# Queries and keys written twice before their transposes, and a shorter inverse root, in a hybrid decoder step

## The chip, the cores and the metric

The kernel runs on one core of a Trainium2 chip. The metric is the device time of one execution in microseconds. Times inside a profile count from the start of its span. The engines are called TensorE (PE in the rows; PEld is its weight load), VectorE (DVE), ScalarE (ACT), GpSimd (POOL) and SP, which issues most of the transfers.

## What is computed

One layer for 1,024 prompt tokens and 8 x 4 sample tokens of width 1,024. A root-mean-square norm feeds one input projection to queries, keys, values, a gate and the inputs of a state-space branch; the two branches' outputs go through one output projection and are added to the input. The change lies in the attention branch: four heads, each with two softmax maps of 64 columns, whose queries and keys are normed each for itself:

```python
q = _rmsnorm(q.reshape(b, L, N_HEADS, 2, QK_DIM), q_g)
k = _rmsnorm(k.reshape(b, L, N_HEADS, 2, QK_DIM), k_g)
s = jnp.einsum('bqhcd,bkhcd->bhcqk', q, k) * (QK_DIM ** -0.5)
...
w = p[:, :, 0] - lam * p[:, :, 1]
```

The normed keys are also an output of the layer.

## The kernel before, in words

Matrix products are made with operands split into a high and a low part: a 32-bit number is written to a narrower format (fp32r) by ScalarE and the remainder by VectorE, and high x high, high x low and low x high are summed by TensorE in PSUM.

The program has three stages. The first (`first_phase`) norms the tokens and runs the state-space branch; `stats` (L288) there makes the inverse root of each token's mean square. The second goes through the four heads. The third is the output projection (`out_proj`), whose first row blocks are mixed with the last head's attention.

In the second stage `project` runs, for each head, over four steps of 256 tokens (j = 0 to 3). Each step makes 48 matmuls of 128x512 into two PSUM tiles `acc` (three exist): columns 0 to 255 are the queries and keys of the head's two maps, then values and gate. `norm_qk` (L832) takes both tiles: sums of squares on ScalarE, the inverse root `rsqrt` (L155) on VectorE, and the multiply from PSUM into the tile `qn` (L848). Some time later `keep_qkv` (L899), here called a keep, turns `qn` by transposes on TensorE (L907) into a PSUM tile `tr`, of which two exist, and writes the step's tile `pt`: for each map the scaled query's high part and low part, each on partitions 0 to 63 and again on 64 to 127, and the keys with their high part on one half of the partitions and their low part on the other (L916 to L921). So one matmul of contraction 128 gives high x high + high x low. The plain keys `kf` go out by a transfer (L922).

The attention of the same and the previous head is interleaved with this by hand: `mix` draws from generators by rates and delays given in microseconds of an estimate, and a scheduler then orders each engine's queue by its own estimate of durations. `scores` multiplies `pt` tiles into the PSUM tiles `sc` (two), adds the bias and takes the minimum on VectorE (L1030), the exponential on ScalarE (L1035), and joins the two maps (L1040). `values` transposes the joined weights (L1055, tile `tr`), copies them out (L1058) and multiplies by the values (tile `pv`). `attn_norm` norms the result with another `rsqrt` (L1084 writes `o`), `attn_out` transposes it (L1091, tile `tr`). `sample_attend` does the eight sample groups with paged keys and values. Weights of the next head are split meanwhile, the low parts in turn on VectorE and GpSimd (L183). Each engine takes its queue in order.

The functions that the diff touches, and what calls them:

Of the kernel before, what the change touches and what calls it, by code (L numbers as in the profile page):

```python
# [9 lines left out]
F32 = mybir.dt.float32  # L10
F32R = mybir.dt.float32r
I32 = mybir.dt.int32
AF = mybir.ActivationFunctionType
OP = mybir.AluOpType
# [10 lines left out]
QD = 64  # L25
# [4 lines left out]
BIG = 1e30  # L30
NBUCK = 32
# [95 lines left out]
class Kernel:  # L127
# [27 lines left out]
    def rsqrt(self, out, x, tmp):  # L155
        v = self.nc.vector
        v.tensor_scalar(tmp.bitcast(I32), x.bitcast(I32), 1, None, op0=OP.logical_shift_right)
        v.tensor_scalar(out.bitcast(I32), tmp.bitcast(I32), -1, 0x5F3759DF, op0=OP.mult, op1=OP.add)
        for _ in range(3):
            v.scalar_tensor_tensor(tmp, out, -0.5, out, op0=OP.mult, op1=OP.mult)  # L160
            v.tensor_tensor(tmp, tmp, x, op=OP.mult)
            v.scalar_tensor_tensor(out, tmp, 1.5, out, op0=OP.add, op1=OP.mult)
# [669 lines left out]
    def norm_qk(self, accs, n, ve):  # L832
# [4 lines left out]
        qn = self.att.tile([128, 2, 256], F32, name="qn", tag="qn", bufs=2)  # L837
# [9 lines left out]
        for i, a in enumerate(accs):  # L847
            v.tensor_tensor(qn[0:n, i].rearrange("p (c d) -> p c d", d=QD), a[0:n, 0:256].rearrange("p (c d) -> p c d", d=QD),  # L848
                            r[0:n, 4 * i:4 * i + 4][:, :, None].to_broadcast([n, 4, QD]), op=OP.mult)
        return qn  # L850

    def project(self, w):
# [3 lines left out]
        for h in range(NH):  # L856
            st = {"ga": {}, "PT": {}, "V": {}, "kept": {}, "out": set()}
            self.heads.append(st)
            for j in range(4):
# [25 lines left out]
                qn = self.norm_qk(accs, 128, [self.xe[:, 2 * j + i:2 * j + i + 1] for i in range(2)])  # L885
# [13 lines left out]
    def keep_qkv(self, h, j, qn, vo, st):  # L899
        nc = self.nc  # L900
        v, g = nc.vector, nc.gpsimd
        pt = st["PT"][j] = self.pt("pt")
        nc.sync.dma_start(self.O["v_p"][256 * j:256 * j + 256, 128 * h:128 * h + 128].rearrange("(i p) c -> p i c", i=2), vo)
        qk = self.tr()
        for x in range(2):
            for i in range(2):
                nc.tensor.transpose(qk[:, 256 * x + 128 * i:256 * x + 128 * i + 128], qn[:, i, 128 * x:128 * x + 128], self.idn)  # L907
        q, k = qk[:, 0:256], qk[:, 256:512]
        kf = self.att.tile([128, 256], F32, name="kf", tag="kf", bufs=1)
        half = [slice(64 * c, 64 * c + 64) for c in range(2)]  # L910
        with self.tc.high_priority(HP2):

            for c, ps in enumerate(half):
                hi, lo, kk = (pt[:, 512 * z + 256 * c:512 * z + 256 * c + 256] for z in range(3))
                ot = half[1 - c]
                nc.scalar.activation(hi[ps], q[ps], AF.Copy, scale=self.gains[ps, 0:1])  # L916
                v.tensor_copy(hi[ot], hi[ps].bitcast(F32))  # L917
                v.scalar_tensor_tensor(lo[ps], q[ps], self.gains[ps, 0:1], hi[ps].bitcast(F32), op0=OP.mult, op1=OP.subtract)  # L918
                v.tensor_copy(lo[ot], lo[ps].bitcast(F32))
                nc.scalar.activation(kk[half[0]], k[ps], AF.Copy, scale=self.pkc("k_g")[ps])  # L920
                v.scalar_tensor_tensor(kk[half[1]], k[ps], self.pkc("k_g")[ps], kk[half[0]].bitcast(F32), op0=OP.mult, op1=OP.subtract)  # L921
            nc.scalar.activation(kf, k, AF.Copy, scale=self.pkc("k_g"))  # L922
        nc.sync.dma_start(self.O["kT"][h, :, 256 * j:256 * j + 256], kf)
        st["kept"][j] = self.clock
# [424 lines left out]
def _build(arrays):  # L1349
    import concourse.bacc as bacc  # L1350

    nc = bacc.Bacc("TRN2", target_bir_lowering=False, num_devices=1)
# [29 lines left out]
```

## Time and profile before

| what | value |
|---|---|
| median of three runs | 678.12 us (677.19 to 678.22) |
| profiled execution | 676.66 us |
| its span | 674.9 us |
| mean granted clock of TensorE | 0.944 of full speed |
| busy, TensorE, VectorE, ScalarE, GpSimd | 595.2, 489.1, 313.7, 160.2 us |

Busy time is the union of the times that an engine's instructions were shown as running, over the whole span. A matmul's shown time overlaps that of the next one, so the rate of a row of matmuls is read from starts, or from the chain of waits, and not from their mean duration. The chain of waits is followed back from the last instruction; each piece is either work or the wait that ended last. The span is 1.76 us shorter than the profiled execution's time, and that execution 1.46 us shorter than the median.

### The profile page before, as it was taken

How to read it: one execution, taken by the hardware profiler on the slowest of the kernel's cores; microseconds unless marked ns; L12 is line 12 of the kernel's file. 1: busy time of each engine (PE TensorE's matmuls, PEld its weight loads, DVE VectorE, ACT ScalarE, POOL GpSimd, SP SyncE). 2: the span in 40 equal slices, each digit the busy share in tenths (PEclk: the TensorE clock that was granted, in tenths of full speed). 3: DMA queues.
4: the chain of work that ended last, by engine and by line, in shares of the span. 5: the costliest groups of instructions: out<-in, count | busy, mean ns of one | idle time of the engine just before them, and what ended most of it. 6: DMA issues, size and time to landing. Idle time of an engine off the chain costs nothing.

```text
span 674.9 us, 11323 instructions
## 1 busy us (share of the span) xinstructions
PE 595.2 (88%) x3490; PEld 493.2 (73%) x3490; DVE 489.1 (72%) x1639; ACT 313.7 (46%) x984; POOL 160.2 (24%) x165
## 2 busy tenths in 40 slices
PE   5927679568698999989999899998999989999997
PEld 4926579568687887768877688776887757887775
DVE  5978998899775337899668996689966899922111
ACT  6952332121363336676456764567645677411000
POOL 0681679777524400030000300003000020001000
PEclk9967779797978999999999999999999998999999
DMA  9754408352256450243002530024300166333221
GB/s 305 264 157 130 103 21 219 99 158 67 87 189 171 156 169 17 62 142 110 24 25 62 146 105 25 26 61 146 105 17 31 55 188 214 110 120 124 83 82 51
DMA packets 85738, 74.64 MB, mean 111 GB/s; under 512 B 8685, under 2 KB 74766, under 8 KB 85678
## 3 DMA queue, kind: packets, MB, share of 16 engines
q1 hardware_dynamic: 83374, 69.51, 34.0%
q10 hardware_dynamic: 2304, 4.41, 1.8%
q8 instruction: 28, 0.46, 0.3%
q14 instruction: 32, 0.26, 0.1%
HBM read 53.85 MB, written 20.04 MB: 109 GB/s over the span
## 4 chain that ended last, share of the span: by engine, by line
PE 44%; DVE 30%; ACT 7%; DMA 7%; POOL 6%; issue 5%; SPq 1%; POOLq 0%; DVEq 0%; ACTq 0%
PE acc L135 30%; PE sc L135 5%; PE pv L135 4%; DVE s L1030 3%; DMA xtok<-in_x 2%; DVE ws L183 2%; PE tr L1055 2%; DVE pt L918 2%; DMA gz<-gsd 1%; DVE pt L921 1%; PE tr L135 1%; POOL gz L477 1%; DVE E_im L511 1%; DVE et L507 1%; DVE pt L917 1%
## 5 line engine op out<-in xcount | busy, mean ns | idle before, releaser
L135 PE MATMUL acc<-ws,xt 128*128 128x512 f32 x768 | 204.5, 403 | 0.2 <-DVE gz L501 0.2
L135 PEld LDWEIGHTS acc<-ws,xt 128*128 128x128 f32 x768 | 137.1, 189 | 25.7 <-issue 1.2
L183 POOL TENSOR_TENSOR ws<-wraw,ws 128x512 fp32r<-128x512 f32 x30 | 46.8, 1563 | 369.4 <-ACT ws L180 289.0
L135 PE MATMUL acc<-xt,ws 128*128 128x352 f32 x576 | 99.3, 332 | 8.0 <-ACT ws L180 8.0
L135 PEld LDWEIGHTS acc<-xt,ws 128*128 128x128 f32 x576 | 95.3, 194 | 10.8 <-ACT ws L180 8.4
L135 PE MATMUL acc<-ws,o 128*128 128x512 f32 x336 | 84.5, 400 | 2.9 <-ACT ws L180 0.9
L135 PEld LDWEIGHTS acc<-ws,o 128*128 128x128 f32 x336 | 63.2, 192 | 17.4 <-ACT ws L180 1.3
L1035 ACT ACTIVATE s<-s,mn 128x128 f32<-128x128 f32 (+7 forms) x64 | 49.6, 778 | 28.7 <-DVE mn L1030 18.8
L135 PE MATMUL sc<-pt 128*128 128x256 f32 (+1 forms) x320 | 58.0, 296 | 5.0 <-DVE mn L1030 2.6
L135 PEld LDWEIGHTS sc<-pt 128*128 128x128 f32 x320 | 46.0, 189 | 21.7 <-DVE mn L1030 5.3
L180 ACT ACTIVATE ws<-wraw 128x512 fp32r<-128x512 f32 x68 | 41.8, 627 | 34.5 <-PE acc L135 22.5
L1264 DVE TENSOR_TENSOR xres<-acc,xres 128x512 f32<-128x512 f32 x16 | 11.0, 690 | 51.8 <-PE acc L135 51.8
L135 PE MATMUL pv<-vo,wt 128*128 128x128 f32 x288 | 42.0, 284 | 0.0
L135 PEld LDWEIGHTS pv<-vo,wt 128*128 128x128 f32 x288 | 37.9, 196 | 4.0 <-ACT wt L1058 1.9
L183 DVE TENSOR_TENSOR ws<-wraw,ws 128x512 fp32r<-128x512 f32 x38 | 31.7, 837 | 6.2 <-ACT ws L180 6.1
L405 ACT ACTIVATE acc<-gs 128x352 f32<-128x352 f32 x12 | 5.6, 468 | 61.3 <-DVE gs L404 61.3
L135 PE MATMUL acc<-z,ws 128*128 128x352 f32 x144 | 25.9, 340 | 4.4 <-DVE gs L406 2.7
L135 PEld LDWEIGHTS acc<-z,ws 128*128 128x128 f32 x144 | 24.7, 199 | 5.6 <-DVE gs L406 2.9
L1055 PE MATMUL tr<-cn,s 128*128 128x128 f32 x144 | 26.9, 279 | 1.3 <-ACT kf L922 1.3
L840 ACT ACTIVATE qn<-acc 128x64 f32<-128x64 f32 x128 | 26.8, 225 | 0.0
L1030 DVE CUSTOM_DVE_ANT_0 s<-sc,cb 128x512 f32<-128x512 f32 (+3 forms) x48 | 26.3, 549 | 0.5
L1040 DVE SCALAR_TENSOR_TENSOR s<-s,ls 128x128 f32<-128x128 f32 (+7 forms) x32 | 26.0, 813 | 0.3
(281 smaller groups left out, 1084.1 us busy)
## 6 DMA issues: line engine op xcount, KB each, us to landing
wraw<-in_w_in SPq DMA_DIRECT2D x44, 256.0 KB, 3.2
xT<-in_xT SPq DMA_DIRECT2D x12, 352.0 KB, 7.3
xtok<-in_x SPq DMA_DIRECT2D x8, 512.0 KB, 5.3
cached<-in_cache_k SPq DMA_DIRECT2D x64, 64.0 KB, 1.9
cached<-in_cache_v SPq DMA_DIRECT2D x64, 64.0 KB, 1.9
wraw<-in_w_out SPq DMA_DIRECT2D x16, 256.0 KB, 2.9
xres<-in_x SPq DMA_DIRECT2D x16, 256.0 KB, 3.0
out_y<-xres SPq DMA_DIRECT2D x16, 256.0 KB, 2.0
```

The source lines that it names most:

```text
L135: self.nc.tensor.matmul(out, lhsT, rhs, start=start, stop=stop)
L180: nc.scalar.activation(hi, raw, AF.Copy)
L183: (nc.vector if self.turn else nc.gpsimd).tensor_tensor(lo, raw, hi.bitcast(F32), op=OP.subtract)
L477: nc.gpsimd.tensor_tensor(gz, gz, z, op=OP.mult)
L507: eng.tensor_tensor(t1, a_im, b_im, op=OP.mult)
L840: nc.scalar.activation(qn[0:n, i, 64 * c:64 * c + 64], a[0:n, 64 * c:64 * c + 64], AF.Square, accum_out=ss[0:n, 4 * i + c:4 * i + c + 1])
L918: v.scalar_tensor_tensor(lo[ps], q[ps], self.gains[ps, 0:1], hi[ps].bitcast(F32), op0=OP.mult, op1=OP.subtract)
L1030: v.tensor_tensor_reduce(out=s[:, k0 + a0:k0 + a1], in0=q[:, a0:a1], in1=bias, op0=OP.add, op1=OP.min, scale=1.0, scalar=last, accum_out=m)
L1035: nc.scalar.activation(s[:, 0:L], s[:, 0:L], AF.Exp, bias=last, scale=-1.0, accum_out=ls[:, 2 * i + c:2 * i + c + 1])
L1040: v.scalar_tensor_tensor(wv, st[1][:, 0:L], cf, wv, op0=OP.mult, op1=OP.add)
L1055: nc.tensor.transpose(q[:, 128 * b:128 * b + 128], wv[:, 128 * (b0 + b):128 * (b0 + b) + 128], self.idn)
L1264: v.tensor_tensor(x, a, x, op=OP.add)
```

## The change

`norm_qk` gets a factor `times`. For the prompt it is 2: `qn` has 512 columns per token block in place of 256, each 64-column map standing there twice in a row. A keep makes eight transposes into two PSUM tiles, one for the queries and one for the keys, so that each map stands on both halves of the partitions as it leaves TensorE. The high and low parts of the queries are then written by one instruction each over 128 partitions and 512 columns, the keys by one instruction of that size and one of 64 x 512, and `kf` by two of 64 x 256; the copies from one half of the partitions to the other (L917, L919) are gone. The sample group keeps `times=1`.

`rsqrt` goes from eleven vector instructions to eight: the integer start value in one instruction in place of two, then one Newton step with changed constants and one step of higher order in place of three Newton steps. It is called for the tokens, the queries and keys, the attention's output and the sample groups.

The scratch for dynamic DMAs is set to 2,048 bytes.

```diff
     def rsqrt(self, out, x, tmp):
         v = self.nc.vector
-        v.tensor_scalar(tmp.bitcast(I32), x.bitcast(I32), 1, None, op0=OP.logical_shift_right)
-        v.tensor_scalar(out.bitcast(I32), tmp.bitcast(I32), -1, 0x5F3759DF, op0=OP.mult, op1=OP.add)
-        for _ in range(3):
-            v.scalar_tensor_tensor(tmp, out, -0.5, out, op0=OP.mult, op1=OP.mult)
-            v.tensor_tensor(tmp, tmp, x, op=OP.mult)
-            v.scalar_tensor_tensor(out, tmp, 1.5, out, op0=OP.add, op1=OP.mult)
+        v.tensor_scalar(out.bitcast(I32), x.bitcast(I32), -0.5, float(0x5F1FFFF9), op0=OP.mult, op1=OP.add)
+        v.scalar_tensor_tensor(tmp, out, -RS1, out, op0=OP.mult, op1=OP.mult)
+        v.tensor_tensor(tmp, tmp, x, op=OP.mult)
+        v.scalar_tensor_tensor(out, tmp, RS1 * RS2, out, op0=OP.add, op1=OP.mult)
+        v.scalar_tensor_tensor(tmp, out, RS3, out, op0=OP.mult, op1=OP.mult)
+        v.tensor_tensor(tmp, tmp, x, op=OP.mult)
+        v.scalar_tensor_tensor(tmp, tmp, -1.25 / RS3, tmp, op0=OP.add, op1=OP.mult)
+        v.scalar_tensor_tensor(out, tmp, 1.875, out, op0=OP.add, op1=OP.mult)
...
-    def norm_qk(self, accs, n, ve):
+    def norm_qk(self, accs, n, ve, times=1):
...
-        qn = self.att.tile([128, 2, 256], F32, name="qn", tag="qn", bufs=2)
+        qn = self.att.tile([128, 2, 512], F32, name="qn", tag="qn", bufs=2)
...
         for i, a in enumerate(accs):
-            v.tensor_tensor(qn[0:n, i].rearrange("p (c d) -> p c d", d=QD), a[0:n, 0:256].rearrange("p (c d) -> p c d", d=QD),
-                            r[0:n, 4 * i:4 * i + 4][:, :, None].to_broadcast([n, 4, QD]), op=OP.mult)
+            sh = [n, 4, times, QD]
+            v.tensor_tensor(qn[0:n, i, 0:256 * times].rearrange("p (c t d) -> p c t d", c=4, t=times),
+                            a[0:n, 0:256].rearrange("p (c d) -> p c d", d=QD)[:, :, None, :].to_broadcast(sh),
+                            r[0:n, 4 * i:4 * i + 4][:, :, None, None].to_broadcast(sh), op=OP.mult)
...
-        qk = self.tr()
-        for x in range(2):
-            for i in range(2):
-                nc.tensor.transpose(qk[:, 256 * x + 128 * i:256 * x + 128 * i + 128], qn[:, i, 128 * x:128 * x + 128], self.idn)
-        q, k = qk[:, 0:256], qk[:, 256:512]
+        q, k = self.tr(), self.tr()
+        for x, o in enumerate((q, k)):
+            for c in range(2):
+                for i in range(2):
+                    y = 128 * (2 * x + c)
+                    nc.tensor.transpose(o[:, 256 * c + 128 * i:256 * c + 128 * i + 128], qn[:, i, y:y + 128], self.idn)
...
+        hi, lo, kk = (pt[:, 512 * z:512 * z + 512] for z in range(3))
         with self.tc.high_priority(HP2):
+            nc.scalar.activation(kk, k, AF.Copy, scale=self.pkc("k_g"))
+            nc.scalar.activation(hi, q, AF.Copy, scale=self.gains[:, 0:1])
+            low = kk[half[1]]
+            v.scalar_tensor_tensor(low, k[half[1]], self.pkc("k_g")[half[1]], low.bitcast(F32), op0=OP.mult, op1=OP.subtract)
+            v.scalar_tensor_tensor(lo, q, self.gains[:, 0:1], hi.bitcast(F32), op0=OP.mult, op1=OP.subtract)
             for c, ps in enumerate(half):
-                hi, lo, kk = (pt[:, 512 * z + 256 * c:512 * z + 256 * c + 256] for z in range(3))
-                ot = half[1 - c]
-                nc.scalar.activation(hi[ps], q[ps], AF.Copy, scale=self.gains[ps, 0:1])
-                v.tensor_copy(hi[ot], hi[ps].bitcast(F32))
-                v.scalar_tensor_tensor(lo[ps], q[ps], self.gains[ps, 0:1], hi[ps].bitcast(F32), op0=OP.mult, op1=OP.subtract)
-                v.tensor_copy(lo[ot], lo[ps].bitcast(F32))
-                nc.scalar.activation(kk[half[0]], k[ps], AF.Copy, scale=self.pkc("k_g")[ps])
-                v.scalar_tensor_tensor(kk[half[1]], k[ps], self.pkc("k_g")[ps], kk[half[0]].bitcast(F32), op0=OP.mult, op1=OP.subtract)
-            nc.scalar.activation(kf, k, AF.Copy, scale=self.pkc("k_g"))
+                nc.scalar.activation(kf[ps], k[ps, 256 * c:256 * c + 256], AF.Copy, scale=self.pkc("k_g")[ps])
...
-    nc = bacc.Bacc("TRN2", target_bir_lowering=False, num_devices=1)
+    nc = bacc.Bacc("TRN2", target_bir_lowering=False, num_devices=1, dynamic_dma_scratch_size=2048)
```

`project` calls `norm_qk` with `times` = 2. The constants are RS1 = 0.703952253, RS2 = 2.38924456 and RS3 = the root of 0.375.

The scheduler orders the queues anew. Line numbers of the changed kernel are larger by 3 in the helpers and by some 9 in the attention. Two places of the second head follow. TensorE, from the transposes of the keep of j = 2 on; `tr<-cn,qn` are the keep's transposes, `tr<-cn,s` those of the attention's weights, `acc` the projection, `sc` the scores. Before:

```order
L907 MATMUL tr<-cn,qn 128x128 x4
L135 MATMUL acc<-ws,xt_84 128x512 x3
L1055 MATMUL tr<-cn,s 128x128 x2
L135 MATMUL sc<-pt 128x256
L1055 MATMUL tr<-cn,s 128x128 x2
L135 MATMUL acc<-ws,xt_85 128x512 x2
L135 MATMUL sc<-pt 128x256 x3
L135 MATMUL acc<-ws,xt_85 128x512
```

and in the changed kernel:

```order
L919 MATMUL tr<-cn,qn 128x128 x2
L138 MATMUL acc<-ws,xt_89 128x512 x2
L919 MATMUL tr<-cn,qn 128x128 x6
L138 MATMUL acc<-ws,xt_84 128x512 x3
L138 MATMUL sc<-pt 128x256
L138 MATMUL acc<-ws,xt_85 128x512 x2
L138 MATMUL sc<-pt 128x256 x3
L1064 MATMUL tr<-cn,s 128x128 x3
```

The attention's transposes, which stood between the projection and the first scores, now stand behind the scores; two of the keep's transposes stand apart from the other six. From the keep's last transposes to the next ones of the attention's output (`tr<-cn,o`) 35 projection matmuls stood in the queue, now 22.

VectorE at the same keep, from the multiply of `norm_qk` on; `ISA s,mn` is the score's bias and minimum. Before:

```order
L848 TENSOR_TENSOR qn<-acc,qr 128x256 x2
L897 SCALAR_TENSOR_TENSOR ga<-silu,acc 128x128 x2
L917 CAST pt<-pt 64x256
L918 SCALAR_TENSOR_TENSOR pt<-tr,gains,pt 64x256
L919 CAST pt<-pt 64x256
L921 SCALAR_TENSOR_TENSOR pt<-tr,pk,pt 64x256
L1030 ISA s,mn<-sc,cb 128x384
```

and in the changed kernel:

```order
L856 TENSOR_TENSOR qn<-acc,qr 128x512 x2
L906 SCALAR_TENSOR_TENSOR ga<-silu,acc 128x128
L1161 RECIPROCAL sl<-sl 128x1
L1163 TENSOR_SCALAR sp<-sp,sl 128x288
L906 SCALAR_TENSOR_TENSOR ga<-silu,acc 128x128
L929 SCALAR_TENSOR_TENSOR pt<-tr,gains,pt 128x512
L928 SCALAR_TENSOR_TENSOR pt<-tr,pk,pt 64x512
L1039 ISA s,mn<-sc,cb 128x384
```

Before, the four instructions of the second half came again behind that score, among further scores; now the two stand together ahead of it, the queries' low part first.

## Rows read from the trace of the kernel before

**Rows 1.** Page, parts 1 and 4: busy time and chain by engine.

```profile
PE 595.2 (88%) x3490; PEld 493.2 (73%) x3490; DVE 489.1 (72%) x1639; ACT 313.7 (46%) x984; POOL 160.2 (24%) x165
...
PE 44%; DVE 30%; ACT 7%; DMA 7%; POOL 6%; issue 5%; SPq 1%; POOLq 0%; DVEq 0%; ACTq 0%
```

**Rows 2.** Busy time by stage; behind the engines clock, DMA share, GB/s.

```profile
270.57:354.76 84.19, 81.53 (x498) 63.92 (x498) 68.15 (x304) 50.93 (x192) 5.95 (x4) 1.00 0.25 73
523.11:575.00 51.89, 47.54 (x291) 36.50 (x291) 46.67 (x199) 37.48 (x127) 6.80 (x5) 0.93 0.50 155
550.00:555.00 5.00, 3.00 (x42) 1.77 (x43) 4.86 (x17) 3.62 (x13) 1.26 (x1) 1.00 0.79 229
555.00:560.00 5.00, 4.45 (x19) 3.73 (x19) 4.44 (x24) 4.47 (x22) 0.00 (x0) 0.52 0.89 262
```

**Rows 3.** Timeline of TensorE, one head: start, us, instruction, idle before.

```profile
378.75 1.14 PE L135 MATMUL sc<-pt 128*128 128x256 f32 x6 [0.80 <-DVE mn L1030]
...
384.19 0.41 PE L135 MATMUL sc<-ob,cn 128*32 128x128 f32 x2 [0.20 <-ACT ob L1178]
...
387.14 0.33 PE L1091 MATMUL tr<-cn,o 128*128 128x128 f32 x1 [0.72 <-DVE o L1084]
...
422.18 0.49 PE L1091 MATMUL tr<-cn,o 128*128 128x128 f32 x2 [0.31 <-DVE o L1084]
```

**Rows 4.** Chain of waits, one head and last stretch: start, us, what.

```profile
392.72 0.48 ACT pt L916
...
394.56 0.48 DVE pt L921
...
402.94 4.16 PE acc L135 x18
...
412.51 0.87 PE tr L1055 x8
...
559.26 6.21 PE acc L135 x21
```

**Rows 5.** Groups by shape: instruction, count, busy us, mean ns, idle before.

```profile
L135 PE MATMUL acc<-ws,xt 128*128 128x512 f32 x768 | 204.5, 403 | 0.2 <-DVE gz L501 0.2
...
L921 DVE SCALAR_TENSOR_TENSOR pt<-tr,pk,pt 64x256 fp32r<-64x256 f32 x32 | 15.5, 484 | 4.4 <-ACT pt L920 3.8
L918 DVE SCALAR_TENSOR_TENSOR pt<-tr,gains,pt 64x256 fp32r<-64x256 f32 x32 | 15.4, 483 | 0.8
L920 ACT ACTIVATE pt<-tr,pk 64x256 fp32r<-64x256 f32 x32 | 15.0, 469 | 21.7 <-DVE pt L918 21.6
...
L1058 ACT ACTIVATE wt<-tr 128x512 f32<-128x512 f32 x24 | 13.8, 592 | 3.7 <-PE tr L1055 3.7
...
L848 DVE TENSOR_TENSOR qn<-acc,qr 128x256 f32<-128x256 f32 x32 | 12.1, 418 | 0.6
...
L1264 DVE TENSOR_TENSOR xres<-acc,xres 128x512 f32<-128x512 f32 x16 | 11.0, 690 | 51.8 <-PE acc L135 51.8
...
L907 PE MATMUL tr<-cn,qn 128*128 128x128 f32 x64 | 10.7, 274 | 0.0
...
L919 DVE CAST pt<-pt 64x256 fp32r<-64x256 f32 x32 | 10.2, 319 | 1.1
...
L917 DVE CAST pt<-pt 64x256 fp32r<-64x256 f32 x32 | 9.2, 288 | 13.7 <-ACT pt L916 13.3
...
L160 DVE SCALAR_TENSOR_TENSOR qt<-qr 128x8 f32<-128x8 f32 x48 | 7.8, 163 | 0.7
```

**Rows 6.** Timeline of VectorE and TensorE, token norms at the start.

```profile
48.57 2.53 DVE L160 SCALAR_TENSOR_TENSOR xtmp<-xr 128x9 f32<-128x9 f32 x1
...
52.03 0.17 DVE L160 SCALAR_TENSOR_TENSOR xtmp<-xr 128x9 f32<-128x9 f32 x1
...
54.66 3.86 PE L135 MATMUL tr<-diag,ones 128*128 128x384 f32 x6 [16.82 <-DVE diag L307]
```

**Rows 7.** Page of the profile, part 3: the first DMA queue.

```profile
q1 hardware_dynamic: 83374, 69.51, 34.0%
```

More of the change, by code (lines that the diff above doesn't have):

```diff
@@ L30 @@
 BIG = 1e30
+RS1, RS2 = 0.703952253, 2.38924456
+RS3 = math.sqrt(0.375)
 NBUCK = 32
@@ L884, in project @@
                         due.append((self.clock + DUE, lambda h=h, qn=qn, st=st: self.keep_sample(h, qn, st)))
-                qn = self.norm_qk(accs, 128, [self.xe[:, 2 * j + i:2 * j + i + 1] for i in range(2)])
+                qn = self.norm_qk(accs, 128, [self.xe[:, 2 * j + i:2 * j + i + 1] for i in range(2)], 2)
                 for i in (0, 1):
```

## Prediction

> **What bounds the kernel now.** I read the shares of the engines first, then the busy time by stage, then TensorE's own order of work in one head. The page says that TensorE is busy for 88% of the span and that 44% of the chain that ended last runs over it, 30% over VectorE [rows 1]. The stage table puts the change's place at 270 to 575 us: three heads alike, of which the first row stands for all: 84.19 us, TensorE busy for 81.53 of them, VectorE for 68.15, ScalarE for 50.93; and a last stretch in which the output projection begins [rows 2]. So TensorE binds in the heads, with small holes. The timeline shows where: before 378.75, 387.14 and 422.18 us it stood idle 0.80, 0.72 and 0.31 us, each time for VectorE, before 384.19 us 0.20 for ScalarE; three shorter holes make up the rest of 2.66 us a head [rows 2, 3]. A matmul's shown duration runs past the start of the next one: 403 ns is shown where eighteen in a row take 4.16 us, 0.231 each [rows 4, 5]. A hole is therefore some 0.17 us longer than shown, and seven holes make 2.66 + 1.2 = 3.9 us a head, 11.6 us in three heads.
>
> The last stretch is looser: 51.89 us with 47.54 busy, 4.35 idle, VectorE at 46.67 [rows 2]. [...] **All holes together: 11.6 + 4.35 + 1.4 = 17.3 us.** That is what a lighter VectorE can give back at most in this stage.
>
> **The change part by part.** *TensorE.* Each of the 16 keep steps (four per head) has 8 transposes in place of 4: 64 more. Eight transposes of 128x128 in a row take 0.87 us [rows 4], 0.109 each: 64 x 0.109 = **+7.0 us** on the engine that binds. Nothing hides it but a hole it happens to fall in.
>
> The mean duration shown for such a transpose is 274 ns [rows 5], but that counts time in which the next one already runs. [...]
>
> *VectorE in the keep step.* Eight instructions of 64 rows by 256 go per keep, two each of 288, 319, 483 and 484 ns [rows 5]: 3.15 us. Two of 512 columns come. No row has this operation at 512 columns; from below it is the 690 ns of an addition of 128x512 out of PSUM, from above 483 + 272 = 755 ns, 272 being what 256 more columns cost between the two rows of additions out of PSUM (418 and 690) [rows 5]. I take 0.755, the same operation's own base. Per head: -12.6 + 6.0.
>
> *VectorE in the norm.* The multiply out of PSUM goes from 256 to 512 columns, 8 per head, +0.272 each: +2.2 us. The inverse root loses three of its eleven instructions, ten times per head (four norms of queries and keys, four of the attention's output, two of the sample group): 30 x 0.163 = -4.9 us [rows 5]. From the sums of squares to the written query, three steps fewer (-0.5) and two longer multiplies (+0.54) cancel, so the transposes can't begin earlier by this part. In sum VectorE has -12.6 + 6.0 + 2.2 - 4.9 = **-9.3 us of 68.15 per head**.
>
> *ScalarE.* Five instructions go per keep (2.35 us at 469 ns); two of 128x512 come, between 0.59 (the row of that size without a factor) and 0.74 (469 + 272), say 0.65, and two copies of 64x256 at 0.47: 2.24 us [rows 5]. That changes nothing, on an engine busy for 51 of 84 us.
>
> *The keep's chain.* Before, one half of a keep goes over ScalarE, VectorE, VectorE, ScalarE and VectorE in turn, 392.72 to 395.04 us, and the other half does the same behind it [rows 4]: some 4.6 us until queries and keys are whole. Now the high part is written in 0.65, the low part in 0.755 after it, and the keys' pair runs beside: about 2.2 us. The scores wait for it.
>
> *Start of the kernel.* The inverse root of the token norms is on the path: TensorE waits 16.82 us for what is made of it [rows 6]. Its ordinary steps take 0.17 us, one took 2.53 [rows 6]. Three ordinary ones fewer are -0.5; if a long one is among them, up to -3; if the long ones stay and swallow the gap, nothing. I take -0.5.
>
> *The smaller scratch for dynamic DMAs.* 0: the queue with 83,374 packets is a hardware queue [rows 7], and the program issues its transfers on SP and ScalarE, none on GpSimd.
>
> **How much of the 17.3 us goes.** Not all: the order printed above shows that TensorE's instructions were laid closer after the shortened chain (22 projection matmuls between a keep and the next transposes of the output, where there were 35), so slack is spent in advance. VectorE loses 14% of its work, and the three longest holes, 1.83 of 2.66 us, end on it. I take half in the heads, -5.8. In the last stretch VectorE is busy 46.67 of 51.89 us and loses 2 x 1.64 in two keeps and 3 x 0.49 in three roots, less 0.54 in a norm: 4.2 us; the holes there follow it nearly one to one, and with them the low clock: -4.0. **Sum: +7.0 - 5.8 - 4.0 - 0.5 = -3.3 us.** The profiled execution took 676.66 us, 1.46 below the median of 678.12; -3.3 on the median is **674.8 us**. Bounds: no hole goes, +6.5 (684.6); all go, -17.3 + 7.0 - 0.5 = -10.8 (667.3).
>
> **The rivals.** *All holes close.* For it: the holes end on VectorE, which gets 9.3 us of room a head for 3.9 us of holes, and the keep's chain is half as long. Against: the tighter order, and the holes that ScalarE ends. 667.3 us; I count what lies more than 7 us below the median here.
>
> *The new transposes wait for PSUM.* Queries and keys now take both banks of the two for transposes at once; before they took one, and the attention's transposes went on in the other, directly behind them in TensorE's queue. In the new order these come after three projections, one score, two projections and three scores: 5 x 0.231 us, and the four scores, half as wide, at half of that: 1.6 us. If they need the bank of the keys, it is free only 2.2 us after the transposes, and TensorE, which takes its queue in order, stands 0.6 us with everything behind. At twelve keeps in the midst of heads that is 7.2 us: 7.0 - 9.8 + 7.2 - 0.5 = +3.9, **682.0 us**. It decides from 4.7 us of new waits in all (3.3 to use up the gain, 1.4 to show), 0.3 a keep. For it: the first two transposes now stand apart from the other six, so a bank is already awaited. Against: the low part frees the bank of the queries after 1.45 us, inside the cover.
>
> *Break-even.* A third of the holes goes: -17.3/3 - 0.5 + 7.0 = +0.7, 678.8 us.
>
> [...]
>
> **How the numbers follow.** This kernel's runs spread by 0.15%, so 0.2% (1.36 us) is about what a measurement can tell from no change. Chances: forecast (1.4 to 7 us gained) 0.42; all holes close 0.17; break-even 0.16; PSUM waits 0.21; clock 0.04. Faster 0.59, same 0.16, slower 0.25. The range runs from the close of all holes, 667, to the PSUM case, 682, and leaves out about 0.1 at either end.
>
> **What would show it.** Right: 64 more transposes at 0.11 us; VectorE 58 to 60 us busy per head; a head of about 83.9 us with 1 to 2 us idle; the stretch with the low clock gone or shorter; pairs of 0.75 us on VectorE and 0.65 on ScalarE in a keep. Wrong: heads over 85 us with waits of TensorE for a transpose's bank (rival two), heads under 82 (rival one), VectorE's 512-column instructions well over 0.8 us, or the clock below 1.00 inside a head.

## The result, and the profile after

The changed kernel takes **680.66 us** (median of 7 runs, 679.10 to 683.92) where the kernel before takes 677.47 beside it (7 runs, 676.37 to 678.22): ratio 1.0054, interval 1.0029 to 1.0080. It is 3.2 us slower; 674.8 was forecast. The profiled execution took 683.92 us, the slowest of its seven, with a span of 681.7 (before: 674.9), so differences between the two profiles are larger than those between the medians.

The page, parts 1 and 4:

```profile
PE 600.3 (88%) x3554; PEld 499.5 (73%) x3554; DVE 455.5 (67%) x1420; ACT 315.7 (46%) x968; POOL 161.2 (24%) x165
...
PE 54%; DVE 21%; DMA 8%; POOL 5%; ACT 5%; issue 5%; SPq 1%; POOLq 0%; DVEq 0%; ACTq 0%
```

VectorE lost 33.6 us of its 489.1, and the chain that ended last left it for TensorE, 44% to 54% [rows 1]: so far the change did what it was to do. The groups by shape (instruction, count, busy us, mean ns, idle before) have the sizes that were forecast:

```profile
L856 DVE TENSOR_TENSOR qn<-acc,qr 128x512 f32<-128x512 f32 x32 | 20.6, 686 | 0.6
L919 PE MATMUL tr<-cn,qn 128*128 128x128 f32 x128 | 18.6, 281 | 0.0
...
L928 DVE SCALAR_TENSOR_TENSOR pt<-tr,pk,pt 64x512 fp32r<-64x512 f32 x16 | 12.1, 757 | 0.5
L929 DVE SCALAR_TENSOR_TENSOR pt<-tr,gains,pt 128x512 fp32r<-128x512 f32 x16 | 12.0, 750 | 14.4 <-ACT pt L926 14.4
...
L926 ACT ACTIVATE pt<-tr,gains 128x512 fp32r<-128x512 f32 x16 | 11.0, 688 | 4.1 <-PE tr L919 3.7
```

The time went elsewhere. Busy time by stage (columns as in [rows 2]; a head is cut here from the transposes of the keep of j = 1 to the same transposes a head later, which before is 84.36, 84.18 and 84.17 us):

```profile
264.51:350.14 85.63, 82.11 (x514) 64.98 (x513) 60.26 (x250) 51.61 (x186) 5.72 (x4) 1.00 0.25 71
350.14:434.95 84.81, 81.87 (x514) 64.96 (x513) 59.16 (x250) 51.52 (x186) 5.77 (x4) 1.00 0.25 72
434.95:521.58 86.63, 83.32 (x514) 66.06 (x513) 60.49 (x250) 51.67 (x186) 5.29 (x4) 0.98 0.24 69
...
466.40:471.00 4.60, 4.05 (x39) 2.92 (x39) 3.29 (x14) 2.65 (x5) 0.00 (x0) 0.63 0.21 61
```

VectorE needs 59.16 us in the second of them instead of 68.15, and yet the heads are longer, by 1.3, 0.6 and 2.5 us. That is 4.4 of the 6.8 us by which this span is longer than that of the kernel before; 1.2 us lie ahead of these heads and 1.2 behind. In each there is one hole that the kernel before did not have. TensorE's timeline (start, us, instruction, idle before):

```profile
382.13 0.50 PE L138 MATMUL sc<-pt 128*128 128x256 f32 x2 [1.94 <-DVE mn L1039]
382.47 1.33 PE L138 MATMUL acc<-ws,xt 128*128 128x512 f32 x5
...
466.95 0.58 PE L138 MATMUL sc<-pt 128*128 128x256 f32 x2 [1.93 <-DVE mn L1039]
467.32 2.34 PE L138 MATMUL acc<-ws,xt 128*128 128x512 f32 x5
```

The second pair is the same place a head later. TensorE waits there for the minimum of a score tile, and VectorE's timeline shows what stands in front of that minimum:

```profile
378.98 0.15 DVE L163 SCALAR_TENSOR_TENSOR s<-s 128x2 f32<-128x2 f32 x1
380.63 0.91 DVE L1138 TENSOR_TENSOR sbias<-cn,sbias 128x32 f32<-128x32 f32 x1 [1.50 <-DMA sbias<-tbd]
...
381.60 0.47 DVE L1039 CUSTOM_DVE_ANT_0 s<-sc,TB,mn 128x256 f32<-128x256 f32 x1
```

GpSimd's timeline beside it:

```profile
380.23 1.26 POOL L190 TENSOR_TENSOR ws<-wraw,ws 128x512 fp32r<-128x512 f32 x1 [5.44 <-ACT ws L187]
```

Of the 2.2 us that VectorE loses at the addition, 1.50 are the wait for its load. The other 0.73 are the addition's own: it takes 0.91 us where it takes 0.18 in the kernel before, and GpSimd runs a split of weights beside it (the last section has more of this). No run below parts the two.

L1138 is in `sample_attend`, which no line of the diff touches. For each head that function loads the samples' bias rows into a tile `sbias` with a single buffer (L1136, before L1127) and makes a masked copy of four columns with one addition on VectorE (L1138, before L1129), for the next head, which reads it some 70 us later. The load stands in SP's queue behind the value loads of the sample group, and in the new order also behind the keys' store:

```profile
376.85 0.37 SPq L932 DMA_DIRECT2D out_kT<-kf  x1
...
377.79 0.55 SPq L1136 DMA_DIRECT2D sbias<-tbd  x1
```

In the kernel before, the same load (SP) was issued earlier and the addition (VectorE) stood later:

```profile
374.54 0.54 SPq L1127 DMA_DIRECT2D sbias<-tbd  x1
...
382.33 0.18 DVE L1129 TENSOR_TENSOR sbias<-cn,sbias 128x32 f32<-128x32 f32 x1
```

7.79 us lie between the two, where a transfer of this kind lands after 2.8 (median of four, in both traces). In the changed kernel VectorE comes to the addition at about 379.1, 1.3 us after the issue. The scheduler orders the queue by its own estimates; with fewer instructions on VectorE the addition's place is reached sooner (it is the 34th instruction of VectorE's trace behind the buffer's last use, before it was the 56th), and everything behind the addition waits in the queue. The next head's chain of waits (start, us, what) passes through it, and behind the hole TensorE ran the five projections of 467.32 in 2.34 us where the five of 382.47 took 1.33; the granted clock was 0.63 on average from 466.40 to 471.00:

```profile
462.10 2.99 DMA sbias<-tbd
...
465.11 1.25 DVE sbias L1138
```

### The profile page after: what moved, and what is told of

Its sections match the earlier page's. It is cut to its first block, busy times and chain, and to the rows that moved or that the text cites. A ratio compares the mean times of both kernels' runs of the same rounds, so it can differ in the third digit from the quotient of the medians.

```text
span 681.7 us, 11227 instructions
## 1 busy us (share of the span) xinstructions
PE 600.3 (88%) x3554; PEld 499.5 (73%) x3554; DVE 455.5 (67%) x1420; ACT 315.7 (46%) x968; POOL 161.2 (24%) x165
## 4 chain that ended last, share of the span: by engine, by line
PE 54%; DVE 21%; DMA 8%; POOL 5%; ACT 5%; issue 5%; SPq 1%; POOLq 0%; DVEq 0%; ACTq 0%
PE acc L138 38%; PE sc L138 6%; PE pv L138 4%; PE tr L1064 2%; DVE ws L190 2%; PE tr L919 2%; DMA sbias<-tbd 1%; DMA xtok<-in_x 1%; PE tr L138 1%; DMA wraw<-in_w_out 1%; DMA xT<-in_xT 1%; DVE s L1039 1%; DVE E_im L518 1%; DMA wraw<-in_w_in 1%; DVE E_re L513 1%
## 5 line engine op out<-in xcount | busy, mean ns | idle before, releaser
L138 PE MATMUL acc<-ws,xt 128*128 128x512 f32 x768 | 207.8, 406 | 0.2 <-DVE gz L508 0.2
L190 POOL TENSOR_TENSOR ws<-wraw,ws 128x512 fp32r<-128x512 f32 x30 | 47.1, 1575 | 376.7 <-ACT ws L187 374.3
L138 PE MATMUL acc<-xt,ws 128*128 128x352 f32 x576 | 101.5, 337 | 9.1 <-ACT ws L187 9.1
L138 PEld LDWEIGHTS acc<-xt,ws 128*128 128x128 f32 x576 | 97.4, 198 | 11.9 <-ACT ws L187 9.5
L138 PE MATMUL sc<-pt 128*128 128x256 f32 (+1 forms) x320 | 53.7, 291 | 7.7 <-DVE mn L1039 5.8
L190 DVE TENSOR_TENSOR ws<-wraw,ws 128x512 fp32r<-128x512 f32 x38 | 31.6, 833 | 12.0 <-ACT ws L187 11.9
L138 PE MATMUL pv<-vo,wt 128*128 128x128 f32 x288 | 39.0, 278 | 0.0
L138 PEld LDWEIGHTS pv<-vo,wt 128*128 128x128 f32 x288 | 36.0, 191 | 3.9 <-ACT wt L1067 2.6
L1049 DVE SCALAR_TENSOR_TENSOR s<-s,ls 128x128 f32<-128x128 f32 (+7 forms) x32 | 27.5, 861 | 0.4
L905 ACT ACTIVATE silu<-acc,xh 128x128 f32<-128x128 f32 x32 | 11.8, 367 | 34.6 <-DVE qn L856 34.6
```

What stands on the lines that cost most here:

```text
L138: self.nc.tensor.matmul(out, lhsT, rhs, start=start, stop=stop)
L190: (nc.vector if self.turn else nc.gpsimd).tensor_tensor(lo, raw, hi.bitcast(F32), op=OP.subtract)
L905: self.nc.scalar.activation(e, x, AF.Tanh, scale=half_r)
L1049: v.scalar_tensor_tensor(wv, st[1][:, 0:L], cf, wv, op0=OP.mult, op1=OP.add)
```

## Experiments

Each group (1 to 4, 5 to 8, 9 to 12, 13 to 16, 17 and 18) ran beside the kernel before on one chip, another one for each group; the kernel before took 676.87 to 677.27 us there, so a difference between groups is uncertain by some 0.4 us more. Times are medians, in brackets the interval of the ratio. Theory A is the wait just shown. Against it stand B (the 64 transposes are the price) and others that the texts name.

**1. The roots alone.** The kernel before with the new `rsqrt`, nothing else.

> The kernel before with the eight-step inverse roots alone: no added transposes, keep_qkv as before. Theory A (the vector queue's new order is the cost: the bias addition for the samples stands earlier and waits there for its load, some 2.1 us in each of three heads): the order of this kernel has the addition 36 rows behind the last use of the buffer where before had 53, so the stall should show here too, and the time stays within 2 us of before (675.5 to 679.5) although some 4.9 us of vector work a head are gone. Theory B (the 64 added transposes are the cost, 7 us): this kernel has none of them, so the time falls by 2 to 4 us (673.5 to 675.5). Theory C (the two parts simply add up, roots gain): as B.

677.20 us, ratio 0.9997 (0.9973 to 1.0020). The time is A's: VectorE is busy 477.1 us, 12.0 less, and nothing is gained. The wait is not: the addition waits 1.7 us for its load in all, not some 2.1 in each of three heads, and run 10 gains nothing without it.

**2. The doubling alone.** The changed kernel with the old `rsqrt`.

> The changed kernel with the old eleven-step inverse roots: doubling alone. Theory A (the early bias addition): the addition stands 36 rows behind the last use here as well; the stall of about 2 us a head shows, and the time is 680 to 684. Theory B (the 64 transposes): plus 7 for the transposes less what the shorter keep chain closes, 681 to 685, without a stall at the bias addition. The sum of the time differences of this run and of the roots alone tells whether the two parts add (theory C: the sum is +3.2 within 1.5).

681.28, 1.0054 (1.0035 to 1.0073), and the addition waits 2.9 us. The two parts' differences sum to +3.9, near the whole change's +3.2; this alone does not part A from B.

**3. The addition on GpSimd.**

```diff
-            v.tensor_tensor(new.rearrange(...), same..., bias..., op=OP.add)
+            g.tensor_tensor(new.rearrange(...), same..., bias..., op=OP.add)
```

> The changed kernel with one edit: the samples' bias addition runs on GpSimd, so VectorE no longer waits for that load; order of TensorE unchanged. Theory A: the holes of 2.1 us in the three heads go, and with them the low clock behind the last of them (1.6 us): the time falls by 5 to 8 us, to 673 to 676, head periods near 83.5. Theory B (the transposes are the price, the hole is covered elsewhere): the time stays at 679 to 682, and the wait turns up at another place. A half-way result (676 to 679) means that the hole is real but another wait ends right behind it.

676.79, 0.9989 (0.9968 to 1.0010): 3.9 us below the change. The holes of 1.9 us are gone; GpSimd now waits for the load, 17.2 us in all.

**4. The load issued by ScalarE.**

```diff
-            nc.sync.dma_start(bias[:, 0:132], self.bias_rows(h))
+            nc.scalar.dma_start(bias[:, 0:132], self.bias_rows(h))
```

> The changed kernel with one edit: the load of the samples' bias rows is issued by ScalarE, not behind 12 value loads and a key store in SyncE's queue; the addition stays on VectorE (it moves up 23 rows, to right behind the buffer's last use, in the planner's order). Theory A: the load lands some 10 us earlier, but the addition also stands earlier; where the load takes 2.8 us, as on SyncE, a short wait of 0 to 1.5 us a head remains, and the time is 673 to 678. Theory B: 679 to 682.

674.75, 0.9961 (0.9942 to 0.9980): 5.9 us below the change, faster than the kernel before. The heads of this run:

```profile
345.19:428.30 83.11, 81.78 (x515) 65.01 (x513) 60.07 (x250) 51.45 (x186) 5.14 (x4) 1.00 0.26 74
428.30:511.73 83.43, 81.90 (x515) 64.99 (x514) 61.05 (x250) 51.37 (x186) 5.14 (x4) 1.00 0.24 72
```

One argument of one instruction makes the heads 1.7 and 3.2 us shorter, at the same work; in the heads the addition waits once, 0.29 us in the first. B is out as the cause of the loss.

**5 to 7. The same load in the kernels without the whole change.** The edit of run 4 on the kernel before, on the roots alone and on the doubling alone.

> The kernel before with the load of the samples' bias rows issued by ScalarE. Theory A (the gain of the fourth run is the wait that the change had brought): before had no such wait (0.2 us in all), so nothing is gained: 676.5 to 678.5. Rival D (the other issuer is itself worth 6 us in any of these kernels, since SyncE's queue is relieved): 671 to 673.

676.25, 0.9981 (0.9966 to 0.9996): 0.8 us below the kernel before, measured beside it. D falls; the edit is worth little where there was no wait.

> The eight-step roots alone with the load from ScalarE. Theory A: without the wait (1.7 us in the run of the roots alone) their gain comes out, 673 to 676. Theory E (the roots are worth nothing because keep's chain, not VectorE's sum, bounds the heads without the doubling): 676 to 678.

680.89, 1.0038 (1.0014 to 1.0061), a miss for both theories as put. Its VectorE timeline shows that the order moved the addition into a keep, and that the wait came back there, 1.93 us in the third head. That this alone is why A's number failed is not shown, for run 10 has no gain either:

```profile
457.75 0.19 DVE L1136 TENSOR_TENSOR sbias<-cn,sbias 128x32 f32<-128x32 f32 x1 [1.93 <-DMA sbias<-tbd]
```

> Doubling with the old roots and the load from ScalarE. Theory A: the wait gone (2.9 us and what followed), 676 to 679. If the two parts add, this run and the one of the roots with the same load differ from the kernel before, with the same load, by amounts whose sum is that of the fourth run (674.75) within 1.5.

679.46, 1.0028 (1.0008 to 1.0048); of 2.3 us of waiting at the addition 2.0 lie ahead of the heads. The parts do not add: +4.6 and +3.2 against run 5, and -1.5 for both together.

**8. Half the transposes.** As run 4, with four transposes a keep.

```diff
-            for c in range(2):
+            for c in range(1):
                 for i in range(2):
                     y = 128 * (2 * x + c)
...
-            nc.scalar.activation(kk, k, AF.Copy, scale=self.pkc("k_g"))
+            nc.scalar.activation(t2(kk), t2(k), AF.Copy, scale=self.pkc("k_g"))
```

(`t2` reads the 256 columns twice; the other reads of the two tiles are changed in the same way.)

> As the fourth run, with only four of the eight transposes of each keep: the second map is left out, and the first one is read twice, so outputs of the second map are not computed; every ACT and VectorE instruction keeps its size. It prices the 64 added transposes. If TensorE bounds the heads, as the forecast had it: 64 times 0.109, 7 us, less the last head's part that holes hide, so 667.5 to 669.5. Theory F (the heads are bound by waits on VectorE also now): 672 to 675. [...]

666.95, 0.9842 (0.9816 to 0.9868): 7.8 us below run 4. The three heads of its trace:

```profile
261.86:343.29 81.43, 79.98 (x499) 63.76 (x498) 60.58 (x250) 51.36 (x186) 5.65 (x4) 1.00 0.27 75
343.29:425.28 81.99, 80.15 (x498) 63.78 (x497) 60.69 (x250) 51.24 (x186) 5.67 (x4) 1.00 0.27 75
425.28:507.19 81.91, 80.38 (x499) 63.77 (x498) 60.49 (x250) 51.33 (x186) 5.72 (x4) 1.00 0.25 73
```

Run 4 has 83.64, 83.11 and 83.43 us there, 4.85 us more for 48 transposes, 0.10 each. The rest of the 7.8 us lies behind these heads, and run 8's profiled execution also has a higher granted clock (0.959 on average over the span against 0.949), so 7.8 / 64 = 0.122 is more than a transpose costs. Without the wait TensorE does bind, busy for 79.98 of 81.43 us in the first of these heads, and the term was rightly sized; F is out.

**9 to 12. Four buffers.** All loads and additions come ahead of the heads; on the changed kernel, on each part and on the kernel before (the last three with the smaller scratch where they had not had it).

```diff
-            bias = self.att.tile([128, 164], F32, name="sbias", tag="sbias", bufs=1)
+            bias = self.att.tile([128, 164], F32, name="sbias", tag="sbias", bufs=4)
```

> The changed kernel with four buffers for the samples' bias rows instead of one: all four loads and additions are issued ahead of the heads, and no head has one. Order of TensorE and VectorE otherwise the same. Theory A: the wait cannot arise; 673 to 675.5, like the load from ScalarE, with head periods of 83 to 83.5. Theory B (the price is the transposes and the other issuer did something else): 679 to 682.

676.16, 0.9983 (0.9971 to 0.9996): 4.5 below the change. No head has a wait for the load, and the first stretch of the heads pays a little (0.8 us of waiting at the additions).

> The eight-step roots alone, four buffers for the bias rows (and the smaller DMA scratch that makes room for them). The run of the roots with the load from ScalarE still waited at the addition (3.2 us in two heads) and fell 2.4 us behind in one place. Theory A: the wait was what ate the roots' gain; without it 674 to 676. Theory E (the roots are worth nothing without the doubling): 676.5 to 678.

679.23, 1.0035 (1.0020 to 1.0050). A's number missed again, and here without any wait in a head: the roots alone are worth nothing or less. E is nearer, though not in its range. TensorE's longest holes in the second head, 0.83 us before 378.74 and 1.21 before 389.28, come right behind these VectorE steps, beside GpSimd's splits of 376.76 to 378.05 and 387.10 to 388.38; alone each takes some 0.15 us:

```profile
376.93 1.15 DVE L164 TENSOR_TENSOR s<-s 128x2 f32<-128x2 f32 x1
...
387.20 1.19 DVE L168 SCALAR_TENSOR_TENSOR s<-s 32x1 f32<-32x1 f32 x1
```

> Doubling with the old roots, four buffers. Theory A: 676 to 678, below the 681.3 of doubling alone by what the wait cost there (2.9 us and what followed). Doubling alone is then worth about nothing by itself: 7 to 8 us of transposes against the holes that the shorter keep chain closes.

678.78, 1.0019 (1.0002 to 1.0035): 2.5 below the doubling alone, and still not a gain. VectorE is held beside GpSimd's splits here too, in the second head for 1.08, 1.26 and 1.11 us at three short steps.

> The kernel before with four buffers and the smaller DMA scratch. Theory A: nothing to gain but what the load from ScalarE brought before (0.2 per cent): 676 to 677.5. It is also the control for the scratch: were the smaller scratch itself a cost, 678 to 680.

678.07, 1.0017 (1.0003 to 1.0031). The buffers and the smaller scratch are no gain by themselves; against this run the whole change is worth -1.9.

**13 to 16. The last stretch.** The forecast took 4.0 us from the stretch where the last head hands over to the output projection, and there nothing came. From the last head's keep of j = 1 to the end, before and in the changed kernel:

```profile
515.99:674.90 158.91, 149.25 (x779) 117.73 (x777) 81.23 (x296) 55.15 (x167) 11.45 (x8) 0.98 0.34 110
```

```profile
521.58:681.70 160.12, 150.24 (x791) 118.34 (x789) 77.11 (x254) 55.17 (x164) 10.66 (x8) 0.98 0.34 109
```

TensorE is idle for 9.66 us before and 9.88 after, and in run 4 for 10.34 of 160.90. In run 4 from 550 to 560 us:

```profile
550.00:555.00 5.00, 1.14 (x4) 0.30 (x2) 4.69 (x15) 3.40 (x15) 2.54 (x2) 0.99 0.78 227
555.00:560.00 5.00, 4.49 (x15) 3.64 (x16) 4.86 (x15) 3.48 (x9) 0.00 (x0) 0.50 0.83 243
```

TensorE is idle 3.86 us of the first five, in which VectorE is busy for 4.69, and 0.51 of the next five. What VectorE does there, in its timeline, and GpSimd's beside it:

```profile
549.95 0.15 DVE L165 SCALAR_TENSOR_TENSOR s<-s 32x1 f32<-32x1 f32 x1
...
550.16 1.24 DVE L166 SCALAR_TENSOR_TENSOR s<-s 32x1 f32<-32x1 f32 x1
...
552.87 1.16 DVE L163 SCALAR_TENSOR_TENSOR qt<-qr 128x8 f32<-128x8 f32 x1
```

```profile
550.12 1.26 POOL L190 TENSOR_TENSOR ws<-wraw,ws 128x512 fp32r<-128x512 f32 x1 [2.61 <-ACT ws L187]
552.74 1.28 POOL L190 TENSOR_TENSOR ws<-wraw,ws 128x512 fp32r<-128x512 f32 x1 [1.35 <-ACT ws L187]
```

A step of one column takes 1.24 us, until GpSimd's weight split ends (550.16 + 1.24 = 551.40; 550.12 + 1.26 = 551.38), and the next split does the same. The chain of waits runs through both steps to TensorE's start at 555.51. The split of weights (`split_w`, L190, before L183) goes to VectorE and GpSimd in turn. Run 13 gives all of GpSimd's 30 to VectorE (17 of them between 240 and 600 us), 14 holds the first reloaded tile in memory that is free earlier, 15 does both, 16 repeats run 4. Each is an edit of run 4.

```diff
         if self.turn is not True:
-            self.turn = 1 if not self.turn else 0
+            self.turn = 1
...
-        self.o = [self.fp.tile([128, 2, S], F32R, name="o%d" % i) for i in range(7)]
+        self.o = [(self.att if i == 3 else self.fp).tile([128, 2, S], F32R, name="o%d" % i) for i in range(7)]
```

> The fourth run's kernel (load from ScalarE) with every weight split of the heads on VectorE, none on GpSimd. VectorE's small steps took 1.1 to 1.3 us where a split ran on GpSimd beside them, and 0.15 elsewhere. Theory G (those steps are what holds the handover): two such places in the handover, 2.2 us less there against two splits of 0.68 more, so 673.0 to 674.5 if the rest is unchanged. Theory H (the reload of the attention output holds it, whatever VectorE does): within 0.8 of the fourth run. Theory T (TensorE bounds the heads): VectorE may do 16 splits, 11 us, more over the heads and the heads stay within 0.5 us each.

668.96, 0.9872 (0.9853 to 0.9891): **8.3 us below the kernel before** and 5.9 below run 16, more than G had; with run 15 the fastest that does the whole work. Its heads and the handover:

```profile
347.33:429.70 82.37, 81.46 (x514) 65.52 (x513) 60.63 (x254) 51.85 (x186) 0.00 (x0) 1.00 0.26 74
...
548.00:553.00 5.00, 2.92 (x21) 2.03 (x19) 4.36 (x24) 4.58 (x27) 0.00 (x0) 1.00 0.77 229
553.00:558.00 5.00, 4.63 (x15) 3.34 (x15) 4.61 (x17) 4.79 (x14) 0.00 (x0) 0.72 0.86 263
```

VectorE does four more splits a head and is busy for 60.63 us, as in run 4 (60.07 and 61.05); the two heads shown for run 4 are 0.7 and 0.9 us shorter, and the handover has 2.45 us idle where run 4 had 4.37. What it got back is seen in the step that joins the two maps (L1049, two operands in SBUF), by shape. In the changed kernel it takes 1,270 ns on average:

```profile
L1049 DVE SCALAR_TENSOR_TENSOR s<-s,ls 128x768 f32<-128x768 f32 x4 | 5.1, 1270 | 0.1
```

In run 4, where one of the four takes 2.03 us from 546.29 on, beside a split of GpSimd from 546.24 to 547.51:

```profile
L1049 DVE SCALAR_TENSOR_TENSOR s<-s,ls 128x768 f32<-128x768 f32 x4 | 7.6, 1895 | 0.1
```

In run 13, without splits on GpSimd, the same step at its own length:

```profile
L1049 DVE SCALAR_TENSOR_TENSOR s<-s,ls 128x768 f32<-128x768 f32 x4 | 4.0, 1008 | 0.0
```

> The fourth run's kernel with the first of the seven reloaded tiles of the output projection in memory that is free before the heads end, so that its loads and splits come at the start of the heads. Theory H (the reload holds the handover): 3 products of 0.23 are possible at once, and the chain of the other six is one load, one copy and one subtraction shorter, 0.5 to 1.5 us: 673.2 to 674.3. Theory G: within 0.5 of the fourth run.

675.72, 0.9978 (0.9963 to 0.9993): nothing gained. H is out: it is not the reload that holds the handover.

> Both edits of the last two. If each works on its own part, their gains add; if both only shorten VectorE's queue at the handover, the larger of the two stands: 672 to 674.

668.79, 0.9873 (0.9848 to 0.9898): the same as run 13.

> The fourth run's kernel again, for the comparison with the three beside it: 674 to 676 by both theories (it measured 674.75, ratio 0.9961).

674.83, 0.9961 (0.9948 to 0.9974), as in the fourth run.

**17 and 18. No splits on GpSimd, the old load.** The first edit of run 13 alone, on the changed kernel and on the kernel before.

> The changed kernel with every weight split of the heads on VectorE, the load of the bias rows as the change left it. If the wait for the bias rows stands by itself: 668.96 (the same with the load from ScalarE) plus 4 to 6, so 673 to 675. If GpSimd's split beside the addition was the larger part of it: 669 to 671.

669.59, 0.9890 (0.9868 to 0.9912), in the range of the second reading, but it does not bear that reading out: with VectorE's order longer by its splits the addition stands late again and waits for nothing:

```profile
383.58 0.18 DVE L1138 TENSOR_TENSOR sbias<-cn,sbias 128x32 f32<-128x32 f32 x1
```

> The kernel before with every weight split of the heads on VectorE. VectorE did 68.15 of 84.2 us a head here, and 4 splits of 0.68 a head replace 4 that it waited out for about 1.1 us: by that 1 to 2 us a head less work, and 672 to 676. If the splits on GpSimd matter only where VectorE has nothing but them to wait for: 676.5 to 679. The difference of 17 to 18 is what the change is worth where GpSimd is out of the way: the forecast's minus 3.3 if its sum was right but for the wait.

672.07, 0.9922 (0.9906 to 0.9938). In this pair neither kernel waits at the addition and neither has GpSimd's splits, and the change is worth 669.59 - 672.07 = **-2.5 us**. With intervals of 1.5 and 1.1 us to either side that is not to be told from the forecast's -3.3. But the holes that GpSimd's splits make, among those that the forecast meant to close, are gone from both kernels here. A head of run 18:

```profile
346.51:429.62 83.11, 81.53 (x498) 63.95 (x497) 67.62 (x308) 50.74 (x190) 0.00 (x0) 1.00 0.26 74
```

## Why the prediction was wrong

**VectorE's -9.3 us a head: right.** It is busy for 59.16 to 60.49 us instead of 68.15 to 68.83, and every size holds: 686 ns for the longer multiply (690 forecast), 750 and 757 for the new pair (755), 688 on ScalarE (650 forecast, between the ends given).

**The 64 transposes, +7.0: right.** Taking them out again gave 0.10 us for each in three heads, 0.109 forecast; the 7.8 us of the whole run hold something else as well.

The changed kernel's trace shows 281 ns as the duration of one transpose; run 8's heads show 0.10 us as what one costs there.

**Half of the holes in the heads, -5.8: this step failed.** The text said that the longest holes end on VectorE, and that a lighter VectorE would close them. Without the new wait holes did close, and more of them than forecast: run 8's heads, which have the lighter VectorE and none of the added transposes, take 81.43, 81.99 and 81.91 us where the kernel before takes 84.36, 84.18 and 84.17, so 2.2 to 2.9 us a head are gone where half of 3.9 was forecast. But the step looked at the new order of TensorE alone. It priced at nothing a wait that the new order brings on VectorE: an addition of 32 columns that now stands 22 instructions sooner while its load is issued later. That wait, the hole that it makes on TensorE, and the lower clock behind one of the holes (0.63) cost 5.9 and 5.8 us by runs 4 and 16, 4.5 by run 9, 3.9 by run 3.

Nor is it shown that holes close because VectorE has less to do. The two longest of a head [rows 3], before 378.75 and 387.14, come right behind two steps that take 0.17 and 0.16 us elsewhere; VectorE, and GpSimd beside it:

```profile
376.84 1.26 DVE L157 TENSOR_SCALAR s<-s 128x2 int32<-128x2 int32 x1
...
385.45 1.24 DVE L1082 TENSOR_TENSOR s<-s,xh 128x2 f32<-128x2 f32 x1
```

```profile
376.72 1.36 POOL L183 TENSOR_TENSOR ws<-wraw,ws 128x512 fp32r<-128x512 f32 x1 [4.69 <-ACT ws L180]
...
384.79 1.89 POOL L183 TENSOR_TENSOR ws<-wraw,ws 128x512 fp32r<-128x512 f32 x1 [2.40 <-ACT ws L180]
```

Run 18 takes these splits from GpSimd and leaves VectorE as busy as it was (67.62 us, 68.16 before, in the second head), and TensorE is idle there for 1.58 us instead of 2.65. So the kernel before already lost at VectorE's neighbour part of what the forecast ascribed to VectorE's load.

**The last stretch, -4.0: also wrong.** "The holes there follow it nearly one to one" did not hold: VectorE had 4.1 us less to do there (77.11 for 81.23, the forecast's 4.2), and TensorE was idle for 9.88 us instead of 9.66. What holds that place is when VectorE's short steps get past GpSimd's splits, as 13 (2.45 us idle in ten at the handover, 4.37 in run 4) and 14 (675.72 us, 674.83 in run 16) tell apart; the number of steps matters less. The 1.4 us for the low clock are 6.21 us of 21 products [rows 4] less 0.231 us each, beside a mean granted clock of 0.52 from 555 to 560 us [rows 2] and 0.79 from 560 to 565. No run shows them by themselves; a low clock came again in the changed kernel (0.54 from 565 to 570 us), in run 4 (0.50 from 555 to 560) and in run 13 (0.72 from 553 to 558).

**The start, -0.5: seen, and larger.** Before, 11.68 us lie between the last norm step ahead of the root and TensorE's first product behind it [rows 6], in the changed kernel 10.48:

```profile
42.98 2.13 DVE L292 TENSOR_SCALAR xv<-xv 128x9 f32<-128x9 f32 x1 [0.79 <-ACT xtok L274]
```

```profile
45.52 2.05 DVE L299 TENSOR_SCALAR xv<-xv 128x9 f32<-128x9 f32 x1 [0.77 <-ACT xtok L281]
...
56.00 3.95 PE L138 MATMUL tr<-diag,ones 128*128 128x384 f32 x6 [15.70 <-DVE diag L314]
```

Runs 1, 4, 8, 10 and 16, with the shorter root, have 10.47 to 10.55, runs 2, 5, 7 and 12, with the old one, 11.47 to 11.75. Both long steps are still there in the changed kernel (1.11 and 2.53 us, beside GpSimd's work). The place as a whole moves by more than the term between executions, from 53.8 in run 4 to 56.2 in run 16.

**The scratch, 0:** no run shows a gain or a cost that needs it; run 12 has it together with the four buffers, +1.2 us in all (678.07 against 676.87 beside it).

**The sum by its parts.** Run 8 against run 5 is everything but the transposes and the wait: 666.95 - 676.25 = -9.3, where the forecast had -10.3 (-5.8 - 4.0 - 0.5). That the sums are so near is luck in part: by the two traces the three heads gave 6.8 us (5.8 forecast), the last stretch 0.9 (4.0) and what lies ahead of the heads 1.5 (0.5). With +7.8 that is -1.5 for the change without its wait, and with the wait's 5.9, less the 0.8 that run 5 gained, +3.6 against the kernel before; +3.2 was measured. These are differences of the same runs set end to end, so that they close proves nothing more.

**The rivals.** The PSUM rival gave 682.0, the number nearest to the result, for a cause that is not there: the attention's transposes waited for the keys' bank 1.0 us in the whole run (group of the changed kernel), not 7.2:

```profile
L1064 PE MATMUL tr<-cn,s 128*128 128x128 f32 x144 | 26.4, 279 | 1.1 <-ACT kf L931 1.0
```

Of the clock, the rival given 0.04, the changed kernel shows 1.00 in two heads with 16 more transposes each and 0.98 in the third, with 0.63 on average from 466.40 to 471.00, behind the new hole: that rival is out too. Heads over 85 us were named as a sign of a wrong forecast, and two came, 85.63 and 86.63; the wait named with it was the wrong one.

**What stays open.** The two parts do not add: with the load from ScalarE each alone is a loss (runs 6 and 7, run 6 with a wait left in a head), with four buffers each alone is +1.2 and +0.7 against run 12, and both together -1.9. Runs 10 and 11 show no wait for the load in a head, but short steps of VectorE held beside GpSimd's splits; neither part alone was tried without those splits. Nor was it tried why the changed kernel's seven runs spread over 4.8 us where the kernel before spreads over 1.9.

## What to carry to other kernels

Where a scheduler orders the queues by its estimates, a change moves instructions that it never mentions: compare every in-order engine's queue, look there for instructions that wait for a transfer, and ask of each how long after the issue it is now reached. Small operands that depend on nothing can have a buffer each and be made ahead of the loop. And a helper engine that takes half of a cheap job can cost the engine it helps about as much as the job: here a split of 0.68 us on VectorE, given to GpSimd, held VectorE for 0.5 to 0.65 us by the estimate below, and taking all 30 back made the kernel 5.9 us faster (run 13 against run 16). Price it by what its neighbour's steps take beside it.

## What the hardware showed that was not expected

In the traces of the kernel before and of the changed kernel, each VectorE instruction with two operands in SBUF that began between 260 and 620 us while GpSimd ran a split of 128x512 (1.26 us at the shortest) lasted at least until the split ended: 1.22 us for one column (L166 at 560.00 in the changed kernel; 1.24 in run 4, above) instead of 0.15, 0.91 and 1.25 for the addition (380.63 and 465.11) instead of 0.18. In the kernel before a step with one operand, L157 above, was held too: 1.26 us instead of 0.17; another such step, L1038 at 548.29, kept its 0.27. Where VectorE began first, the split was the longer one: L1040 took 1.02 us from 384.51 on, and the split of 384.79 took 1.89. A step that reads PSUM was not held: in the changed kernel the split from 373.51 to 374.79 has this beside it, at the duration that the same step has at 375.80, where no split runs:

```profile
373.94 0.56 DVE L1039 CUSTOM_DVE_ANT_0 s<-sc,cb 128x384 f32<-128x384 f32 x1
...
375.80 0.56 DVE L1039 CUSTOM_DVE_ANT_0 s<-sc,cb 128x384 f32<-128x384 f32 x1 [0.40 <-PE sc L138]
```

In sum, run 13 does 30 splits more on VectorE, 30 x 0.68 = 20.4 us at the duration of one that stands alone, and its VectorE is busy 462.3 us against 457.7 in run 16 and 461.4 in run 4, the same kernel twice: by that, an estimate, 15.8 to 19.5 us of its time, 0.5 to 0.65 us for each split, had been waiting for GpSimd, shown as busy.

Why a step is held beside a split, and why one step with one operand was and another was not, no run here tells.
